# Layer 0 experts: the next expert's gathered rows are transposed and split in steps, one behind each column block of the first product

## The chip, the core and the metric

The kernel runs on one NeuronCore of a Trainium2 chip. The metric is device time in microseconds (us) for one launch; a lower time is better. The engines are PE (matmul), ACT (ScalarE), DVE (VectorE), POOL (GpSimd, here the issuer of gathers and scatters) and SP (SyncE, here the issuer of plain loads). Each runs its own list of instructions in order and waits on the others by semaphores.

## What is computed

The program is a two-layer backbone: per layer a mixer (attention and a second branch) and then an expert-choice feed-forward. Layer 0 serves a latent stream of 1024 tokens and a context stream of 256; layer 1 serves the latent stream alone. The change lies in the experts of layer 0:

```python
def expert_choice_ffn(h, w_router, w1, w3, w2):
    n_tok, d = h.shape[1], h.shape[2]
    cap = EC_FACTOR * n_tok // N_EXPERTS
    aff = jax.nn.softmax(jnp.einsum('bnd,de->bne', h, w_router).astype(jnp.float32), axis=-1)
    gate, idx = lax.top_k(jnp.swapaxes(aff, 1, 2), cap)
    xs = jax.vmap(lambda hb, ib: hb[ib])(h, idx)
    a = jnp.einsum('becd,edf->becf', xs, w1)
    b = jnp.einsum('becd,edf->becf', xs, w3)
    y = jnp.einsum('becf,efd->becd', jax.nn.silu(a) * b, w2) * gate[..., None].astype(h.dtype)
```

There are 16 experts. Each takes the 128 latent tokens (and, in layer 0, 32 context tokens) that score highest for it; the model and the hidden width are 1024. The results are added back to the rows they came from.

## The kernel before

Every fp32 operand is held as two fp16 halves, high and low, and each product is three matmuls (`mm3`, L146 to L148). A weight piece of 128 x 2048 is loaded as fp32 (`raw`, 1 MB, issued by SP in `slab`, L442) and split: ACT writes the high half (L102), DVE the low half (L103), into `spl`. An expert has twelve such pieces, here numbered 0 to 11 in the order of their splits: 0 to 3 and 4 to 7 are w1 and w3 for the first and second half of the hidden columns, 8 to 11 are w2. In layer 0 `raw` has four buffers, used in turn, so the load of piece n can start only when DVE has split piece n - 4. `spl` has ten, so the split of piece n waits until PE is done with piece n - 10. The splits therefore run some six pieces ahead of PE.

`experts` (L458) loops over the experts. For one expert of layer 0 the work on PE is

- the first product in four column blocks, called block 1 to 4 here: per block 48 matmuls into `pa` (w1) and 48 into `pb` (w3), each with 160 columns (128 latent and 32 context tokens). Behind a block ACT and DVE form silu(a) times b (`sa`, L547 and L548) and split it into `gh` (ACT, L114) and `gl` (DVE, L116);
- the second product, 48 matmuls of 512 columns into `y` for the latent tokens (eight hidden blocks k, two halves, three passes), and 48 of four concurrent column groups into `yc` for the context tokens (L590). What follows a matmul with `gl` of block 4 needs that block's split;
- the scaling of `y` into `ysb` (DVE, L572) and the scatters (POOL, L579 and L596).

While one expert runs, `fetch` prepares the next one's input: POOL gathers 128 rows into `xs` (L474, two buffers) and 32 rows into `xc` (L479, one buffer). PE transposes `xs` in two groups of four (`tr`, L160), and `xc` in one group of eight (`trc`, L489). ACT applies the norm's gain and shift to each group while it reads it from PSUM into `xv` (`affine`, L509), and `split_a` makes `xsh` (ACT, L114) and `xsl` (DVE, L116) of it. All three groups go through one PSUM buffer (tag `tr`, one buffer in layer 0) and one buffer `xv`, so a group's transposes cannot start before ACT has read the group ahead.

`fetch` is called once for each expert, in the second half of the hidden columns, ahead of block 3:

```python
                w1, w3 = ws[:2], ws[2:]
                if fh and e + 1 < NE:
                    nxt = fetch(e + 1)
```

The order of the instructions on each engine is not that of the program text: a scheduler with a timeline model of its own places them, with the text's order as priority. So a change of the text at one place can change the order anywhere behind it.

Of the kernel before, what the change touches and what calls it, by code (L numbers as in the profile page):

```python
# [26 lines left out]
NE = 16  # L27
# [28 lines left out]
def weave(*streams):  # L56
    """streams: (generator, expected sum of its yields, start); advances the one that is least far, start and length 1 being
    where and how fast it runs against the others; a stream that yields a function waits until it is true"""
    live = [[st[0], 0.0, float(st[1]), st[2] if len(st) > 2 else 0.0, None] for st in streams]
    while live:  # L60
        s = min((v for v in live if v[4] is None or v[4]()), key=lambda v: v[3] + v[1] / v[2])
        try:
            r = next(s[0])
            s[4] = r if callable(r) else None
            s[1] += 0.0 if callable(r) else r
        except StopIteration:
            live.remove(s)


class Tag:  # L70
    """one tag of a pool with a fixed number of buffers"""
# [8 lines left out]
class Net:  # L80
# [10 lines left out]
    def first(self, g, n):  # L91
        """the generator's instructions before the n traced ahead of them that are ready too"""
        while True:
            with self.tc.high_priority(n):
                r = next(g, None)
            if r is None:
                return
            yield r

# [5 lines left out]
    def load_split(self, src, n, sp, raws, step=1024):  # L105
        """src [128, n] in DRAM -> sp [128, 2, n]"""
# [32 lines left out]
    def stats(self, x, n, junk, tag):  # L139
        """1 / rms of the rows; tag: buffers of its own for each caller that runs beside others"""  # L140
        ss = self.small.tile([P, 1], F32, name="ss" + tag, bufs=2)
        self.S.activation(junk, x, AF.Square, accum_out=ss)
        return self.rstd_of(ss, n, tag)
# [6 lines left out]
    def turn(self, dst, src):  # L150
        """dst [128, n, 128] <- the n blocks of src [128, n * 128] transposed, 2-byte elements"""
        return self.Y.dma_start(dst, src, transpose=True)

    def trans(self, src, n, psum, w=P):
        """src [128, n*w] fp32 -> psum tiles [w, 4, 128]"""
# [34 lines left out]
    def behind(self, ins):  # L190
        """what is traced inside is issued after ins, on its engine"""
        return contextlib.nullcontext() if ins is None else self.tc.issue_after(ins)

    def mod_bank(self, l, i, psum, raws, last=None, n=1024):
        """rows 32g + stream of the bank: columns 512(4i + g) of the modulation of layer l; n: columns of a load"""
# [24 lines left out]
    def mod_cols(self, l, i, g0, psum):  # L220
        """chunks g0, g0 + 1 of a bank with the model's dimension on partitions: psum [128, 4, 128], columns 32(g0 + g) + stream"""
        return self.trans(self.modsb[l, i], 4, psum)[0]

    def mod_AB(self, l, which, psum):
        """per-partition gain and shift [128, 8] of the norm before the mixer (1) or before the experts (2)"""
# [19 lines left out]
    def router(self, l, j, A, B, psum):  # L245
        """router weights with the norm's gain in them, and the row that its shift gives"""
# [12 lines left out]
    def mod_bc(self, l, m, j, dst, psum):  # L259
        """row m of the modulation for stream j on all partitions, over WS"""  # L260
# [7 lines left out]
    def norm_T(self, src, l, j, hi, lo, xs, psum):  # L268
        """hi, lo: [128, 8, 128] views"""
# [18 lines left out]
    def tail(self, l, j, t, src, catT, wout, m2, xd, h2d, aff, psum, c4, t2, cn=None, xin=None, ptr=None):  # L288
        """catT: k -> (hi, lo) [128, 128 tokens]; wout: (k, half) -> (hi, lo); yields its tensor-engine time"""
# [55 lines left out]
    def topk(self, src, n, cap, tag, off=0, alt=None, bufs=0):  # L345
        """largest cap of src [16, n] in falling order and their columns plus off; src is used up; alt: a second buffer, which
        lets the search for columns run beside the next round"""
# [20 lines left out]
    def merge(self, r, l):  # L368
        """largest 128 of two falling lists of 128; on equal values the first list wins"""
# [10 lines left out]
    def slots(self, vals, idf, cap, psum, halves):  # L380
        """per slot: row index and gate [slots, 16]; halves: also the index of half rows, for both halves"""
# [25 lines left out]
    def ring(self, raws, spls, first=()):  # L407
        """buffers for the experts' weights as loaded and split, (pool, tag) of each, no pool: self.ep; first: those for the first loads"""
# [13 lines left out]
    def first_slabs(self, l, a, b):  # L422
        """loads of the weights a .. b before the tokens are chosen"""
# [7 lines left out]
    def split_first(self, a, b, last=None):  # L431
        """their split, beside VectorE, which the choice holds; not before the instruction last"""
# [9 lines left out]
    def slab(self, src, a):  # L442
        """128 x 2048 weights, split: two views [128, a, 2048 / a]"""
# [14 lines left out]
    def experts(self, l, xd, h2d, lat, ctx, hook=None, keep=None, out=None):  # L458
        """lat = (idx, gate, _); ctx = (xdc, h2dc, (idx, gate, idx2)) or None"""
# [7 lines left out]
        def halves(name, i, e):  # L467
            """[128, 8, N] for expert e, in self.ep or in a buffer of the pool keep"""
# [3 lines left out]
        def fetch(e):  # L472
# [3 lines left out]
            xc = None  # L476
            if ctx:
                xc = ep.tile([P, D], F32, name="xc", bufs=1)
                G.indirect_dma_start(out=xc[:CCAP], out_offset=None, in_=ctx[1], in_offset=IOA(ap=ctx[2][0][:CCAP, e:e + 1], axis=0))  # L479
            for h in range(2):  # L480
# [4 lines left out]
                self.split_a(v, hi[:, sl, :CAP], lo[:, sl, :CAP])  # L485
            if ctx:
# [6 lines left out]
            return hi, lo  # L493
# [17 lines left out]
        def rows(fh, w1, w3, xh, xl, gh, gl):  # L511
            """512 of the hidden columns with the tokens on partitions, then transposed and split"""
# [12 lines left out]
        nxt = fetch(0)  # L525
        for e in range(NE):
            xh, xl = nxt
            gh, gl = halves("gh", 2, e), halves("gl", 3, e)
            for fh in range(2):
                ws = [slab(I[n][l, e, fh, kh], 4) for n in ("w1", "w3") for kh in range(2)]  # L530
                w1, w3 = ws[:2], ws[2:]
                if fh and e + 1 < NE:
                    nxt = fetch(e + 1)
                if ctx is None:
                    rows(fh, w1, w3, xh, xl, gh, gl)
                    continue
                for fp in range(2):
# [12 lines left out]
                    self.split_a(sa, gh[:, fsl], gl[:, fsl])  # L550
            if hook and e == NE - 3:
# [48 lines left out]
    def norm_out(self, xs, fg, tag):  # L600
        """the rows of the tiles over their rms, times the gain, in place"""
# [16 lines left out]
    def even(self, xd, xdc, h2d, h2dc, then):  # L618
        nc, tc, V, S, T, G, Y, I = self.nc, self.tc, self.V, self.S, self.T, self.G, self.Y, self.I
        with self.pool("m0") as pm, self.pool("m0p", PSUM) as pp:  # L620
# [56 lines left out]
            def ropes(ps, H, t):  # L677
                """rotated [128, H, 64] fp32, scale undone by the table"""
# [75 lines left out]
            def score(keep, u):  # L754
                """scores of the unit's heads, a bank for each run of blocks, and the transposed probabilities"""
# [38 lines left out]
            def values():  # L794
                """the oldest unit's probabilities times values; after a tile's last ones its heads' outputs"""
# [108 lines left out]
            def att_all():  # L904
                """the scores run two units ahead of the values"""
# [69 lines left out]
    def odd(self, ms, mw, xs, xsc, xd, h2d, W, then):  # L975
# [9 lines left out]
        if True:  # L985
# [4 lines left out]
            def ropes(z, H, t, b):  # L990
                """z [128, H, 32] view, rotated in place"""
# [14 lines left out]
            if True:  # L1006
                with self.pool("m1c") as pc, self.pool("m1cp", PSUM) as pp:
# [20 lines left out]
                    def lowrank(hh, hl, i, t, lat):  # L1028
# [13 lines left out]
                        def low(parts, r, g, n, tag, dst):  # L1042
                            """n columns normalized, split and transposed into dst"""
# [59 lines left out]
            with self.pool("m1zp", PSUM) as pz:  # L1103
# [3 lines left out]
                def conv_all():  # L1107
                    """gated short convolution, channels on partitions; then the output weights"""
# [52 lines left out]
                if True:  # L1161
# [24 lines left out]
                    def score(t, h, i):  # L1186
                        """scores of a head against one block of keys; after the last one the probabilities"""
# [41 lines left out]
                    def values():  # L1229
                        """the oldest block of probabilities times values; after a tile's last one its heads' outputs"""  # L1230
# [20 lines left out]
                    def att_all():  # L1251
                        """the scores run LA heads ahead of the values"""
# [32 lines left out]
                    def tails():  # L1285
                        """output products and what follows, each tile's buffer for its rows in one of two tags"""
# [128 lines left out]
def pack(x, c, ctx, c_ctx, mod_w, mod_b, norm1_g, norm2_g, ev_w_in, ev_sink, ev_sgu_norm_g, ev_sgu_w, ev_sgu_b, ev_w_out, od_w_in,  # L1415
# [5 lines left out]
    def kpack(w, kt):  # L1421
        """[kt*128, n] -> [128, kt*n]"""
# [54 lines left out]
```

## Time and profile before

| | us |
|---|---|
| median of 3 runs | 2750.52 |
| lowest and highest run | 2747.89, 2755.91 |
| span of the profiled execution, first to last instruction | 2750.4 |
| PE busy | 2361.6 (86%) |
| DVE busy | 2036.0 (74%) |
| ACT busy | 1678.1 (61%) |
| POOL busy | 337.3 (12%) |

No other time is given for the profiled execution than its span; it lies 0.1 us under the median. The program falls into stages: modulation and the layer 0 mixer up to about 700 us, the experts of layer 0 from there to 1428 us, the mixer of layer 1 to about 2165 us, and the experts of layer 1 to the end. A share of busy time over the whole span mixes these.

### The profile page before, as it was taken

What the parts mean: (1) busy time and instruction counts of PE and PEld (TensorE: products, weight loads), DVE (VectorE), ACT (ScalarE), POOL (GpSimd) and SP (SyncE); (2) the same over time, 40 slices, a digit from 0 to 9 for tenths busy, and PEclk for the clock granted to TensorE, in tenths of its full rate; (3) what the DMA queues carried; (4) which work ended last, traced back from release to release, by engine and by line L of the source; (5) the groups of instructions that cost most, each with busy time, mean ns of one, the idle gap of its engine ahead of it and who ended that gap; (6) DMA issues with size and microseconds to landing.
All of it is one profiled execution on the core that took longest, in us unless ns stands there. A gap on an engine that the chain in (4) does not pass through costs nothing. (4 is left out here: it accounts for less than half of the span.)

```text
span 2750.4 us, 48542 instructions
## 1 busy us (share of the span) xinstructions
PE 2361.6 (86%) x19075; PEld 1436.0 (52%) x19075; DVE 2036.0 (74%) x3886; ACT 1678.1 (61%) x2750; POOL 337.3 (12%) x198
## 2 busy tenths in 40 slices
PE   5889888864899999999989989988884699999995
PEld 1345555432677777776855645544553244444442
DVE  5466666676677777767857768778778789888887
ACT  4355556514666676767745456656554588777774
POOL 1000000003111111111120000000015111112211
PEclk8999999886899999999999999999986799999998
DMA  8775555473788888887967657878876499999997
GB/s 309 218 171 118 123 106 117 93 260 112 267 307 285 323 286 322 289 319 272 352 204 225 147 124 142 152 137 186 162 187 244 181 371 401 361 366 360 373 370 273
DMA packets 461995, 661.32 MB, mean 240 GB/s; under 512 B 371115, under 2 KB 371419, under 8 KB 411077
## 3 DMA queue, kind: packets, MB, share of 16 engines
q1 hardware_dynamic: 439894, 582.81, 66.8%
q0 software_dynamic: 21872, 75.41, 9.4%
q8 instruction: 149, 2.44, 0.4%
q14 instruction: 80, 0.66, 0.1%
HBM read 526.86 MB, written 41.94 MB: 207 GB/s over the span
## 5 line engine op out<-in xcount | busy, mean ns | idle before, releaser
L103 DVE SCALAR_TENSOR_TENSOR spl<-raw,spl 128x2048 f16<-128x2048 f32 x369 | 831.7, 2285 | 149.4 <-ACT spl L102 148.8
L102 ACT ACTIVATE spl<-raw 128x2048 f16<-128x2048 f32 x369 | 690.5, 1910 | 191.7 <-DMA raw<-in_w 73.0
L146 PE MATMUL pb<-xsh,spl 128*128 128x160 f16 x1024 | 222.6, 239 | 0.0
L148 PE MATMUL pb<-xsh,spl 128*128 128x160 f16 x1024 | 222.2, 239 | 0.0
L147 PE MATMUL pb<-xsl,spl 128*128 128x160 f16 x1024 | 222.1, 239 | 0.0
L146 PE MATMUL pa<-xsh,spl 128*128 128x160 f16 x1024 | 215.9, 234 | 0.0
L147 PE MATMUL pa<-xsl,spl 128*128 128x160 f16 x1024 | 215.7, 234 | 0.0
L148 PE MATMUL pa<-xsh,spl 128*128 128x160 f16 x1024 | 215.6, 234 | 0.0
L146 PEld LDWEIGHTS <-spl 128*128 128x128 f16 x2048 | 204.0, 100 | 7.2 <-PE yc L590 5.1
L148 PEld LDWEIGHTS <-spl 128*128 128x128 f16 x2048 | 204.2, 100 | 0.2
L147 PEld LDWEIGHTS <-spl 128*128 128x128 f16 x2048 | 204.0, 100 | 0.2
L146 PE MATMUL y<-spl,gh 128*128 128x512 f16 x512 | 195.2, 383 | 10.2 <-ACT gh L114 10.2
L147 PE MATMUL y<-spl,gh 128*128 128x512 f16 x512 | 195.1, 382 | 0.0
L148 PE MATMUL y<-spl,gl 128*128 128x512 f16 x512 | 189.3, 385 | 4.9 <-DVE gl L116 4.9
L579 POOL DMA_INDIRECT xd<-ysb,idxl x31 | 125.4, 4044 | 529.2 <-DVE ysb L572 503.6
L1212 ACT ACTIVATE pr<-sps,nm 128x512 f32<-128x512 f32 (+1 forms) x192 | 116.7, 611 | 104.2 <-DVE nm L1203 79.5
L146 PE MATMUL po<-vS,pT 128*128 128x64 f16 x976 | 121.9, 198 | 56.7 <-DMA pT<-ps 34.6
L1195 PE MATMUL sps<-kT,qT 128*128 128x512 f16 (+1 forms) x576 | 133.7, 352 | 11.6 <-ACT pr L1212 11.2
L146 PEld LDWEIGHTS <-pT 128*128 128x128 f16 x976 | 92.1, 101 | 89.9 <-DMA pT<-ps 48.6
L1196 DVE TENSOR_REDUCE mx<-sps 128x1 f32<-128x512 f32 (+1 forms) x192 | 112.6, 596 | 33.9 <-PE sps L1195 30.9
L116 DVE TENSOR_TENSOR ps<-pr,ps 128x512 f16<-128x512 f32 (+1 forms) x192 | 111.8, 595 | 34.6 <-ACT ps L114 34.4
L213 PE MATMUL modps<-mslab,cs 128*2 128x512 f32 x384 | 89.4, 681 | 53.1 <-DMA mslab<-in_mod_w 48.6
(439 smaller groups left out, 5957.1 us busy)
## 6 DMA issues: line engine op xcount, KB each, us to landing
raw<-in_w SPq DMA_DIRECT2D x384, 1024.0 KB, 7.6
mslab<-in_mod_w SPq DMA_DIRECT2D x80, 512.0 KB, 5.8
mslab<-in_mod_w SPq DMA_DIRECT2D x8, 1024.0 KB, 9.5
raw<-in_wz SPq DMA_DIRECT2D x12, 512.0 KB, 6.7
raw<-in_wconv SPq DMA_DIRECT2D x24, 256.0 KB, 3.6
xin<-in_x POOLq DMA_DIRECT2D x8, 512.0 KB, 6.1
raw<-in_ev_wo SPq DMA_DIRECT2D x8, 512.0 KB, 3.9
xres<-in_x POOLq DMA_DIRECT2D x8, 512.0 KB, 5.3
```

The source lines that it names most:

```text
L102: self.S.activation(hi, raw, AF.Copy, scale=scale)
L103: self.V.scalar_tensor_tensor(lo, raw, scale, hi, op0=OP.mult, op1=OP.subtract)
L116: self.V.tensor_tensor(lo, src, hi, OP.subtract)
L146: self.T.matmul(ps, lh, rh, start=first, stop=False)
L147: self.T.matmul(ps, lh, rl, start=False, stop=False)
L148: return self.T.matmul(ps, ll, rh, start=False, stop=last).ins
L213: T.matmul(ps[c0:c0 + 2], lhs, slab[:rows, g * 512:(g + 1) * 512], start=False, stop=(k == 8), tile_position=(0, c0))
L579: G.indirect_dma_start(out=xd, out_offset=IOA(ap=lat[0][:, e:e + 1], axis=0), in_=ysb, in_offset=None, compute_op=OP.add)
L1195: T.matmul(ps[:, :w], qT[:, 4 * j + h % 4], kT[:, k, c0:c0 + w], start=j == 0, stop=j == 2)
L1196: V.tensor_reduce(mx[:, i:i + 1], ps[:, :w], axis=AX.X, op=OP.max)
L1212: S.activation(pr[:, :w], sp[i][:, :w], AF.Exp, bias=nm, scale=SC1, accum_out=dn[:, i:i + 1])
```

## The change

`fetch` becomes a generator with four steps: the two gathers, the first group of `xs`, the second group of `xs`, the group of `xc`. The loop makes it when an expert starts and takes one step behind each of the four column blocks. In layer 1 (`ctx is None`) it is still drained in one go at the old place. The change also drops docstrings and comments, so the line numbers of the two versions differ by up to seven (L509 becomes L511, L489 L492, L548 L554, L572 L579).

```diff
-        def fetch(e):
+        def fetch(e, got):
+
             xs = ep.tile([P, D], F32, name="xs", bufs=2)
             G.indirect_dma_start(out=xs, out_offset=None, in_=h2d, in_offset=IOA(ap=lat[0][:, e:e + 1], axis=0))
             hi, lo = halves("xsh", 0, e), halves("xsl", 1, e)
-            xc = None
+            got.append((hi, lo))
             if ctx:
                 xc = ep.tile([P, D], F32, name="xc", bufs=1)
                 G.indirect_dma_start(out=xc[:CCAP], out_offset=None, in_=ctx[1], in_offset=IOA(ap=ctx[2][0][:CCAP, e:e + 1], axis=0))
+            yield
             for h in range(2):
                 ps, = self.trans(xs[:, h * 512:(h + 1) * 512], 4, ztr)
                 v = ep.tile([P, 4, P], F32, name="xv", bufs=1)
                 affine(ps, v, 0, 4 * h, 4, CAP)
                 sl = slice(4 * h, 4 * h + 4)
                 self.split_a(v, hi[:, sl, :CAP], lo[:, sl, :CAP])
+                yield
             if ctx:
                 ps = ztr([P, 8, CCAP], "trc")
...
                 self.split_a(v, hi[:, :, CAP:], lo[:, :, CAP:])
-            return hi, lo
...
-        nxt = fetch(0)
+        got = []
+        for _ in fetch(0, got):
+            pass
         for e in range(NE):
-            xh, xl = nxt
+            xh, xl = got.pop(0)
             gh, gl = halves("gh", 2, e), halves("gl", 3, e)
+            nxt = fetch(e + 1, got) if e + 1 < NE else iter(())
             for fh in range(2):
                 ws = [slab(I[n][l, e, fh, kh], 4) for n in ("w1", "w3") for kh in range(2)]
                 w1, w3 = ws[:2], ws[2:]
-                if fh and e + 1 < NE:
-                    nxt = fetch(e + 1)
                 if ctx is None:
+                    if fh:
+                        for _ in nxt:
+                            pass
                     rows(fh, w1, w3, xh, xl, gh, gl)
                     continue
                 for fp in range(2):
...
                     self.split_a(sa, gh[:, fsl], gl[:, fsl])
+                    next(nxt, None)
```

What it does to the order, for one expert in the steady run of the stage. The first place is PE in the first product: the second group `tr` and the group `trc`. Before, and now:

```order
L147 LDWEIGHTS spl
L147 MATMUL pb<-xsl,spl 128x160
L160 MATMUL tr<-c_ident,xs 128x128 x4
L148 LDWEIGHTS spl
L148 MATMUL pb<-xsh,spl 128x160
...
L148 MATMUL pb<-xsh,spl 128x160
L489 MATMUL trc<-c_ident,xc 128x32 x8
L146 LDWEIGHTS spl
L146 MATMUL pb<-xsh,spl 128x160
```

```order
L148 LDWEIGHTS spl
L148 MATMUL pb<-xsh,spl 128x160
L160 MATMUL tr<-c_ident,xs 128x128 x4
L146 LDWEIGHTS spl
L146 MATMUL pa<-xsh,spl 128x160
...
L148 LDWEIGHTS spl
L148 MATMUL pb<-xsh,spl 128x160
L492 MATMUL trc<-c_ident,xc 128x32 x8
L146 LDWEIGHTS gh
L146 MATMUL y_10042<-spl,gh 128x512
```

The first group stands behind block 2 in both. The second stood 65 matmuls later, inside `pb` of block 3, and now stands 96 matmuls later, behind block 3. `trc` stood 12 matmuls into `pb` of block 4 and now stands behind block 4, ahead of `y`.

The second place is ACT over the same stretch, from the splits of piece 11 and of the next expert's piece 0 on. Before, and now:

```order
L102 ACTIVATE spl<-raw 128x2048 x2
L509 ACTIVATE xv<-tr,B_911,A_912 128x128 x4
L102 ACTIVATE spl<-raw 128x2048
L114 ACTIVATE gh<-sa 128x320
L114 ACTIVATE xsh<-xv 128x4x128
L547 ACTIVATE sa<-pa 128x320
L509 ACTIVATE xv<-tr,B_911,A_912 128x128 x4
L114 ACTIVATE gh<-sa 128x320
L102 ACTIVATE spl<-raw 128x2048
```

```order
L102 ACTIVATE spl<-raw 128x2048 x2
L511 ACTIVATE xv<-tr,B_911,A_912 128x128 x4
L114 ACTIVATE gh<-sa 128x320
L102 ACTIVATE spl<-raw 128x2048
L553 ACTIVATE sa<-pa 128x320
L114 ACTIVATE xsh<-xv 128x4x128
L114 ACTIVATE gh<-sa 128x320
L511 ACTIVATE xv<-tr,B_911,A_912 128x128 x4
L102 ACTIVATE spl<-raw 128x2048
```

The two splits still stand ahead of the first `xv`. Block 2's `gh` moves ahead of the next split, and block 3's `gh` ahead of the second `xv`.

The third place is DVE, from the same splits to `gl` of block 4. Before, and now:

```order
L103 SCALAR_TENSOR_TENSOR spl<-raw,spl 128x2048 x3
L116 TENSOR_TENSOR gl<-sa,gh 128x320
L116 TENSOR_TENSOR xsl<-xv,xsh 128x4x128
L548 SCALAR_TENSOR_TENSOR sa<-pb,sa 128x320
L116 TENSOR_TENSOR gl<-sa,gh 128x320
L103 SCALAR_TENSOR_TENSOR spl<-raw,spl 128x2048
L116 TENSOR_TENSOR xsl<-xv,xsh 128x4x128
L548 SCALAR_TENSOR_TENSOR sa<-pb,sa 128x320
L103 SCALAR_TENSOR_TENSOR spl<-raw,spl 128x2048 x3
L116 TENSOR_TENSOR gl<-sa,gh 128x320
```

```order
L103 SCALAR_TENSOR_TENSOR spl<-raw,spl 128x2048 x2
L116 TENSOR_TENSOR gl<-sa,gh 128x320
L103 SCALAR_TENSOR_TENSOR spl<-raw,spl 128x2048
L554 SCALAR_TENSOR_TENSOR sa<-pb,sa 128x320
L116 TENSOR_TENSOR xsl<-xv,xsh 128x4x128
L116 TENSOR_TENSOR gl<-sa,gh 128x320
L103 SCALAR_TENSOR_TENSOR spl<-raw,spl 128x2048
L554 SCALAR_TENSOR_TENSOR sa<-pb,sa 128x320
L103 SCALAR_TENSOR_TENSOR spl<-raw,spl 128x2048
L116 TENSOR_TENSOR xsl<-xv,xsh 128x4x128
L103 SCALAR_TENSOR_TENSOR spl<-raw,spl 128x2048 x2
L116 TENSOR_TENSOR gl<-sa,gh 128x320
```

The same 14 instructions stand there in another order: seven splits, three `gl`, two `xsl`, two `sa`. POOL's order does not change, and SP's loads of the expert weights do not either. In the mixer of layer 1 the scheduler also gives another order: PE, ACT, DVE and SP interleave the scores, the values, the queries and the convolution otherwise from the attention on, with the same instructions. In the last experts of layer 1 a few transposes stand some matmuls earlier or later.

## Rows read from the trace of the kernel before

**Rows 1.** The page: span, busy times, and granted clock in 40 slices.
```profile
span 2750.4 us, 48542 instructions
PE 2361.6 (86%) x19075; PEld 1436.0 (52%) x19075; DVE 2036.0 (74%) x3886; ACT 1678.1 (61%) x2750; POOL 337.3 (12%) x198
PEclk8999999886899999999999999999986799999998
```
**Rows 2.** Busy time by window: experts 0, attention of layer 1, experts 1.
```profile
core 0: us, PE busy (x) PEld busy (x) DVE busy (x) ACT busy (x) POOL busy (x), PEclk, DMA share, GB/s
720.00:1380.00 660.00, 622.99 (x7134) 497.07 (x7133) 497.70 (x395) 464.20 (x590) 108.31 (x55) 0.98 0.85 306
1590.00:2045.00 455.00, 407.05 (x3613) 230.86 (x3612) 346.20 (x907) 287.13 (x712) 5.33 (x10) 0.95 0.77 152
2165.00:2705.00 540.00, 517.73 (x2463) 245.73 (x2462) 466.37 (x298) 416.65 (x394) 96.35 (x28) 0.98 0.97 364
```
**Rows 3.** Waits from 720 to 1380 us: total, times, longest.
```profile
ACT spl L102 <- DMA raw<-in_w: 59.9, 22, 4.9
...
PE tr L160 <- ACT xv L509: 37.0, 13, 3.6
```
**Rows 4.** Timeline of PE: the first group of transposes, experts 1 and 14.
```profile
758.84 0.49 PE L160 MATMUL tr<-c_ident,xs 128*128 128x128 f32 x3
...
1360.18 0.60 PE L160 MATMUL tr<-c_ident,xs 128*128 128x128 f32 x4
```
**Rows 5.** Timeline of PE through one expert (start, length, what, [idle before]).
```profile
886.58 0.24 PE L146 MATMUL pa<-xsh,spl 128*128 128x160 f16 x1
...
899.87 0.60 PE L160 MATMUL tr<-c_ident,xs 128*128 128x128 f32 x4
...
903.63 0.23 PE L146 MATMUL pb<-xsh,spl 128*128 128x160 f16 x1
...
907.73 0.66 PE L160 MATMUL tr<-c_ident,xs 128*128 128x128 f32 x4 [2.76 <-ACT xv L509]
908.22 0.23 PE L148 MATMUL pb<-xsh,spl 128*128 128x160 f16 x1
...
914.61 0.68 PE L489 MATMUL trc<-c_ident,xc 32*128 32x32 f32 x8
...
917.72 0.38 PE L146 MATMUL y<-spl,gh 128*128 128x512 f16 x1
...
928.28 0.39 PE L148 MATMUL y<-spl,gl 128*128 128x512 f16 x1
...
930.11 0.39 PE L590 MATMUL yc<-spl,gl 128*32 128x512 f16 x1
...
931.73 0.24 PE L146 MATMUL pa<-xsh,spl 128*128 128x160 f16 x1
```
**Rows 6.** Timeline of ACT in the same expert.
```profile
902.58 3.71 ACT L102 ACTIVATE spl<-raw 128x2048 f16<-128x2048 f32 x2 [4.06 <-DMA raw<-in_w]
906.19 1.49 ACT L509 ACTIVATE xv<-tr,B,A 128x128 f32<-128x128 f32 x4
907.56 1.92 ACT L102 ACTIVATE spl<-raw 128x2048 f16<-128x2048 f32 x1
909.36 0.47 ACT L114 ACTIVATE gh<-sa 128x320 f16<-128x320 f32 x1
```
**Rows 7.** Timeline of DVE in the same expert.
```profile
919.81 6.68 DVE L103 SCALAR_TENSOR_TENSOR spl<-raw,spl 128x2048 f16<-128x2048 f32 x3
926.41 0.48 DVE L116 TENSOR_TENSOR gl<-sa,gh 128x320 f16<-128x320 f32 x1
```
**Rows 8.** Windows as in rows 2: behind two waits of PE, and this expert.
```profile
862.20:865.60 3.40, 3.40 (x29) 3.40 (x27) 2.90 (x4) 1.69 (x4) 0.89 (x1) 0.50 1.00 414
907.80:911.20 3.40, 3.40 (x48) 3.39 (x49) 2.90 (x2) 2.88 (x4) 1.21 (x1) 1.00 0.95 345
886.58:931.73 45.15, 42.39 (x498) 33.61 (x497) 34.29 (x28) 31.87 (x41) 6.95 (x5) 1.00 0.85 306
```

## The prediction

> **What bounds the kernel now.** I read the page first: PE is busy 86% of a span of 2750.4 us and DVE 74% [rows 1]. That is a mean over stages with different limits, so I took windows next. In the stage that the change touches, the experts of layer 0, PE is busy 623.0 of 660 us, DVE 497.7, ACT 464.2, and the DMA engines 0.85 of the time at 306 GB/s; in the experts of layer 1 the same engines move 364 GB/s at 0.97 [rows 2]. So in layer 0 PE is nearest to its limit, and the loads have room. The view of waits then says what PE waits for there: 13 waits for ACT's `xv`, 37.0 us in all and 3.6 at most, and no other wait of PE of that size [rows 3].
>
> The timelines of one expert show how that wait comes about. Call the start of block 1 time 0 (886.58). PE issues the first group of transposes at 13.29 and would reach the second after a few matmuls more, but stands still for 2.76 us until 907.73, 21.15 on that clock [rows 5]. The second group needs the only PSUM buffer, which ACT empties into `xv`. ACT was late: it waited 4.06 us for a load (piece 11), began that split at 902.58 (16.00), did two splits, and only then `xv`, which ends at 907.68 (906.19 + 1.49) [rows 6]. So PE's wait ends 5.1 us behind the landing of piece 11, whatever PE does in between. That load starts when DVE has split piece 7, early in the same expert.
>
> The waits have a second price. Behind one of them the granted clock is 0.50, that is 1.2 GHz in place of 2.4, and PE is busy all through; behind another, of 2.76 us, it is 1.00 [rows 8]. A stretch of 3.40 us at 0.50 loses 1.7 us of work. From the first group of expert 1 (758.84) to that of expert 14 (1360.18) there are 13 experts in 601.34 us, 46.26 each [rows 4]. PE's own work is 42.39 us in an expert without a fall of the clock [rows 8]. 13 x 42.39 = 551.1, and the 13 waits are 37.0; the 13.3 that remain I put down to the clock.
>
> **The change, part by part.** *Instructions.* None is added or removed on any engine; DMAs are the same, POOL's order too. Only places change, and the order says how.
>
> *First group of transposes:* behind block 2, as before. 0 us.
>
> *Second group.* It now stands behind all of block 3. A `pa` or `pb` takes 3.32 us (from `pb` at 903.63 back to the end of the transposes at 900.31, which start at 899.87 and take 0.44 of issue) [rows 5]. So PE reaches it at 13.29 + 0.44 + 6.64 = 20.37. `xv` is over at 21.10 if ACT's list ahead of it is unchanged, which the order says: the same two splits stand there. The wait is then 21.15 - 20.37 = 0.78 us and not 2.76. Its bounds are 0 (the load comes 0.8 us sooner) and 2.76 (it comes 2.0 later). I take 0.78, as nothing ahead of that load moves by more than a `ysb`.
>
> *The group of `xc`.* It waits for the second `xv`. ACT now has block 3's `gh` ahead of that, which waits for DVE's `sa`, and DVE has the split of the next expert's piece 1 ahead of that `sa`. From ACT's and DVE's rows: `gh` of block 2 takes 0.36 of ACT, the split ends 1.92 later [rows 6], DVE's split 2.2 more (a third of 6.68) [rows 7], `sa`, `xsl` and `xv` some 2.5: the second `xv` ends at about 28.1. PE is done with block 4 at 21.15 + 0.49 + 6.64 = 28.28. No wait, but with 0.2 us to spare; bounds 0 and 1.
>
> *The second product.* This is where the next wait appears. PE needs 0.61 for `trc` and reaches `y` at 28.9, 2.2 us sooner than before (31.14, 917.72) [rows 5]. The last eight matmuls of `y` need `gl` of block 4, which DVE finishes at 926.41 + 0.48 = 926.89, time 40.31, the last of a list that began with the split of piece 11 and holds seven splits [rows 7]. Before, PE came there at 928.28 (41.70), 1.4 us after it [rows 5]. DVE's list from piece 11 to this `gl` holds the same 14 instructions, so I leave its end at 40.31 and allow 0.5 either way for its order. PE now comes at 28.9 plus what lay between `y` and the last eight before (928.28 - 917.72 = 10.56) plus 0.1 for two more `yc` ahead of them: 39.56. New wait: 40.37 - 39.56 = 0.81 us, bounds 0 and 1.5. The cover is thus gone: from here an expert is bound by load, ACT and DVE, not by PE.
>
> *The end of the expert.* Eight `y` take 930.11 - 928.28 = 1.83 and the remaining 23 `yc` about 1.5 (25 took 1.62) [rows 5]: 40.37 + 1.83 + 1.5 = 43.70, against 45.15 before. The mean wait of the 13 is 37.0 / 13 = 2.85 [rows 3], 0.09 more than here, so piece 11 lands that much later on the mean: 43.8.
>
> *The clock.* Before, waits of up to 3.6 us [rows 3] let it fall in some experts. I take it that two waits of 0.8 us, some 19 us apart, leave it at 2.4 GHz: the wait of 2.76 at 907.73 did so already [rows 8]. The other bound is a fall in every expert. It costs 1.7, of which 0.81 goes into the wait for `gl` that follows, so 0.89 x 13 = 11.6 us.
> The Trainium skill's page "TensorE: Matmul & The Clock Gate", section "A second HAM failure mode: psum-queue depth-cycling", tells of a kernel that went through PSUM buffers with small pauses between groups of matmuls, often enough that the clock swung between its levels. That speaks against this change, which puts two small pauses where one long one was; by that rule the sum would end 11.6 us higher. No row read here shows what the clock does behind a wait under 1 us.
>
> *POOL and the scatters.* The gather of `xc` waits for `trc`, now some 0.9 us later in an expert's time, and the scatter of `ysb` is queued behind it. That scatter needs the last `y` anyway, 13 us later. 0 us.
>
> *First and last experts.* Expert 14 had no such wait and expert 15 fetches nothing; expert 0 fetches early in both orders. 0, within 1 us.
>
> *The mixer of layer 1.* Its order changes though its text does not. PE idles 455.0 - 407.05 = 48 us in the attention [rows 2]. Work and dependencies are the same, so the bounds are what the idle time allows: 48 gained, and as much lost if it doubled. I take 0, with 8 us (a sixth of that idle time) either way, as the late parts stand at the same places among the scores in both orders. The experts of layer 1 run at 0.97 of the DMA engines [rows 2], and a few transposes moved by some matmuls do not change their loads: 0.
>
> **Sum.** 13 x (46.26 - 43.8) = 32.0 us, 13.3 of it clock and the rest waits. 2750.4 - 32.0 = 2718.4, and as the median lies 0.1 above the profiled span, **2718.5 us**.
>
> **The rivals.** *PE alone is the limit* (12%): piece 11 lands sooner or DVE's new order ends sooner, and neither wait is left. Then 13 x (46.26 - 42.39) = 50.3 us go: 2700.1. For it: the loads have room [rows 2]. Against: ACT still waits 59.9 us for loads in this stretch [rows 3], and nothing in the change makes them start earlier.
>
> *The clock still falls* (15%): 2718.5 + 11.6 = 2730.1, as worked out above.
>
> *The loads close up* (14%): the new order puts a split between the two halves of `ysb`, so the scatter starts about 2.2 us later and meets the loads of pieces 10 and 11, and an expert's loads have 2.4 us less time. Each us that piece 11 lands later costs an expert 1 us. At 1.5 us later, 2718.5 + 13 x 1.5 = 2738.0; at 2.46 later nothing is gained at all. Against: 0.85 of the DMA engines' time over 45.15 us [rows 8] is 38.4 us, which still goes into 43.8.
>
> *Slower: the attention of layer 1* (6%). Its PE idle time of 48 us nearly doubles under the new interleaving, by 45: 2718.5 + 45 = 2763.5. It decides from 40.3 us of loss on (the 32.0 and 8.3 more). For it: nobody chose that order. Against: the same instructions and the same places for the late work.
>
> That the change does not do what it says is out: the order shows each group behind its block.
>
> **How the numbers follow.** My own case has 47%, and its range, with 8 us for layer 1 and the half us of DVE's order, is 2710 to 2727; 6% is left for mixtures that I did not work out. About 0.3% (8.3 us) is what a measurement of this kernel can tell from no change, so "faster" is below 2742.3 and "slower" above 2758.8. Faster: 46 of my own case, 12, 14 of the clock's 15, 8 of the loads' 14, 3 of the rest: 83%. Same: 10% (5 of the loads, 3 of the rest, 2 of others). Slower: 7% (6 of the attention, 1 of the loads). The range of 2698 to 2741 reaches from just under the case of PE alone to the loads at 1.7 us later.
>
> **What would show it.** Right: the waits of the second group for `xv` fall to about 0.8 us each (some 10 us in all); a wait of PE in `y` for `gl` of about 0.8 appears; 43.8 us from one first group to the next; the split of piece 11 still begins at 16 us; the granted clock in this stage at 0.99 or more; and 1590 to 2045 shifted by 32 us and as long as before. Wrong: second-group waits still above 2 us, piece 11 landing at 17.5 or later, a clock of 0.97 or less, or an attention stage longer by more than 10 us.

## The result, and the profile after

The changed kernel takes 2714.11 us (median of 4 runs, 2708.74 to 2715.35), the kernel before 2752.49 in the same set. The ratio is 0.9843, with a 95% interval of 0.9823 to 0.9862: 38.4 us faster, 4.4 us below the forecast of 2718.5 and inside the range. The profiled execution has a span of 2713.5 us.

The page of the changed kernel, to set against [rows 1]:

```profile
span 2713.5 us, 48543 instructions
PE 2346.0 (86%) x19075; PEld 1421.8 (52%) x19075; DVE 2033.3 (75%) x3886; ACT 1680.0 (62%) x2750; POOL 323.8 (12%) x198
PEclk7999999886899999999989999998985799999998
```

Busy time by window in the changed kernel, as [rows 2]: the experts of layer 0, the attention of layer 1 and the experts of layer 1 (both shifted by about 35 us), and last one single expert.

```profile
core 0: us, PE busy (x) PEld busy (x) DVE busy (x) ACT busy (x) POOL busy (x), PEclk, DMA share, GB/s
720.00:1350.00 630.00, 611.65 (x7187) 486.91 (x7185) 500.43 (x397) 469.88 (x590) 97.07 (x55) 1.00 0.89 322
1555.00:2010.00 455.00, 405.62 (x3611) 228.96 (x3612) 351.81 (x916) 286.91 (x713) 5.33 (x10) 0.95 0.77 152
2131.00:2671.00 540.00, 520.15 (x2482) 246.95 (x2481) 468.05 (x299) 416.35 (x396) 93.96 (x29) 0.99 0.97 364
790.78:834.00 43.22, 42.24 (x497) 33.52 (x497) 34.21 (x28) 32.19 (x41) 6.95 (x4) 1.00 0.89 321
```

The two stages of layer 1 are what they were. In layer 0 the granted clock is now 1.00, and PE idles 18.4 us in 630 where it idled 37.0 in 660. The view of waits from 720 to 1350 us says which waits went and which came:

```profile
ACT spl L102 <- DMA raw<-in_w: 65.5, 30, 4.6
...
PE y L148 <- DVE gl L116: 7.2, 11, 0.7
...
PE tr L160 <- ACT xv L511: 5.3, 7, 1.4
...
PE pb L148 <- DVE spl L103: 2.8, 2, 1.9
...
PE trc L492 <- ACT xv L511: 1.2, 1, 1.2
```

The 37.0 us for `xv` [rows 3] are 5.3; 7.2 us for `gl`, 11 waits of at most 0.7, are new; the some 6 that remain of the 18.4 lie in experts 13 and 14. ACT's own waits for loads did not shrink (59.9 before, 65.5 now): they are as long, but much less of PE's time hangs on them.

From the first group of expert 1 to that of expert 14, as [rows 4], there are now 565.08 us, 43.47 per expert where there were 46.26:

```profile
762.10 0.49 PE L160 MATMUL tr<-c_ident,xs 128*128 128x128 f32 x3
...
1327.18 0.38 PE L160 MATMUL tr<-c_ident,xs 128*128 128x128 f32 x2
```

The timeline of PE through one expert, as [rows 5], with the start of block 1 at 790.78:

```profile
790.78 0.24 PE L146 MATMUL pa<-xsh,spl 128*128 128x160 f16 x1
...
804.07 0.60 PE L160 MATMUL tr<-c_ident,xs 128*128 128x128 f32 x4
...
811.55 0.66 PE L160 MATMUL tr<-c_ident,xs 128*128 128x128 f32 x4 [0.25 <-ACT xv L511]
...
818.78 0.68 PE L492 MATMUL trc<-c_ident,xc 32*128 32x32 f32 x8
...
830.76 0.61 PE L148 MATMUL y<-spl,gl 128*128 128x512 f16 x2 [0.73 <-DVE gl L116]
...
834.00 0.24 PE L146 MATMUL pa<-xsh,spl 128*128 128x160 f16 x1
```

The timelines of ACT and of DVE in the same expert, as [rows 6, 7]:

```profile
806.40 3.71 ACT L102 ACTIVATE spl<-raw 128x2048 f16<-128x2048 f32 x2 [3.69 <-DMA raw<-in_w]
810.01 1.49 ACT L511 ACTIVATE xv<-tr,B,A 128x128 f32<-128x128 f32 x4
...
825.82 4.49 DVE L103 SCALAR_TENSOR_TENSOR spl<-raw,spl 128x2048 f16<-128x2048 f32 x2
830.23 0.48 DVE L116 TENSOR_TENSOR gl<-sa,gh 128x320 f16<-128x320 f32 x1
```

ACT still waits for piece 11 (3.69 us) and splits it from 15.62 on, still does two splits ahead of `xv`, and `xv` still ends 5.1 us behind the landing of piece 11 (810.01 + 1.49 - 806.40). PE now comes there at 20.4 and waits 0.25, not 2.76. The last `gl` ends at 830.71, 24.31 us behind the start of piece 11's split, and PE waits 0.73 for it.

### The profile page after: what moved, and what is told of

Read it like the earlier page. It is cut to its first block, busy times and chain, and to the rows that moved or that the text cites. A ratio compares the mean times of both kernels' runs of the same rounds, so it can differ in the third digit from the quotient of the medians.

```text
span 2713.5 us, 48543 instructions
## 1 busy us (share of the span) xinstructions
PE 2346.0 (86%) x19075; PEld 1421.8 (52%) x19075; DVE 2033.3 (75%) x3886; ACT 1680.0 (62%) x2750; POOL 323.8 (12%) x198
## 5 line engine op out<-in xcount | busy, mean ns | idle before, releaser
L148 PE MATMUL pb<-xsh,spl 128*128 128x160 f16 x1024 | 214.2, 233 | 2.8 <-DVE spl L103 2.8
L146 PE MATMUL pb<-xsh,spl 128*128 128x160 f16 x1024 | 214.4, 233 | 0.0
L147 PE MATMUL pb<-xsl,spl 128*128 128x160 f16 x1024 | 214.2, 233 | 0.0
L146 PEld LDWEIGHTS <-spl 128*128 128x128 f16 x2048 | 200.5, 98 | 6.5 <-issue 5.9
L148 PEld LDWEIGHTS <-spl 128*128 128x128 f16 x2048 | 200.3, 98 | 3.2 <-DVE spl L103 3.2
L147 PEld LDWEIGHTS <-spl 128*128 128x128 f16 x2048 | 200.4, 98 | 0.3
L586 POOL DMA_INDIRECT xd<-ysb,idxl x31 | 115.4, 3723 | 533.4 <-DVE ysb L579 508.9
L1202 PE MATMUL sps<-kT,qT 128*128 128x512 f16 (+1 forms) x576 | 133.0, 354 | 13.3 <-ACT pr L1219 10.8
L146 PEld LDWEIGHTS <-pT 128*128 128x128 f16 x976 | 92.2, 101 | 91.1 <-DMA pT<-ps 48.2
```

What stands on the lines that cost most here:

```text
L146: self.T.matmul(ps, lh, rh, start=first, stop=False)
L147: self.T.matmul(ps, lh, rl, start=False, stop=False)
L148: return self.T.matmul(ps, ll, rh, start=False, stop=last).ins
L586: G.indirect_dma_start(out=xd, out_offset=IOA(ap=lat[0][:, e:e + 1], axis=0), in_=ysb, in_offset=None, compute_op=OP.add)
L1202: T.matmul(ps[:, :w], qT[:, 4 * j + h % 4], kT[:, k, c0:c0 + w], start=j == 0, stop=j == 2)
```

## Where the 38 us came from

Busy time by window over the twelve steady experts, 1 to 12, from the start of a block 1 to the start of another: first in the kernel before (all twelve, then one in which the clock fell), then in the changed kernel.

```profile
745.55:1300.28 554.73, 520.08 (x5954) 414.73 (x5953) 413.22 (x326) 383.45 (x483) 94.17 (x49) 0.98 0.83 301
745.55:792.29 46.74, 43.98 (x497) 35.15 (x496) 34.36 (x28) 31.86 (x41) 8.33 (x5) 0.96 0.82 299
```

```profile
748.81:1266.14 517.33, 506.06 (x5956) 402.22 (x5953) 410.52 (x323) 386.11 (x482) 80.51 (x48) 1.00 0.89 322
```

By the medians the kernel gained 38.4 us; the two profiled executions, on which this part rests, lie 36.9 apart. The twelve take 37.4 us less (46.23 each before, 43.11 now). PE's idle time went from 554.73 - 520.08 = 34.65 to 11.27, which is 23.4 of it; PE's busy time fell by 14.0. Most of the 14.0 is the clock: the expert at 745.55 has the same wait of 2.76 as the one of [rows 5], but the clock falls in it (0.96), and PE is busy 43.98 and not 42.39 [rows 8], so a fall costs 1.59. Seven of the twelve took 46.7 us or more, the other five 45.4 or less: 7 x 1.59 = 11.1. The 2.9 that remain, 0.24 per expert, go with the order of PE's list: in the first run below, where that list is the old one again, PE is busy 42.38 us in an expert with the clock at 1.00 (842.92 to 888.04), as before. Which place in the order it is stays open.

The stage as a whole, from its first `pa` to its last `yc`, is 33.9 us shorter (725.48 to 691.56), because expert 13 took 46.7 as before and expert 14 lost 3.6 us. The two in the kernel before, to set against those of the changed kernel (shown with the run on the weights of layer 1):

```profile
1300.28:1346.89 46.61, 44.24 (x497) 35.12 (x496) 37.65 (x33) 35.58 (x45) 6.17 (x4) 0.96 0.90 325
1346.89:1388.64 41.75, 41.75 (x500) 33.69 (x497) 36.86 (x29) 33.18 (x42) 5.51 (x2) 1.00 0.96 349
```

The rest of the difference lies outside the stage: it began 3.4 us later, and what follows it was 6.4 us shorter. The same changed kernel in a second profiled execution began the stage 4.1 us sooner (701.87 for 706.01), so parts of this size are what two executions differ by.

## The experiments

Theory A: PE's old wait came from the order on ACT. `xv`, which frees the one PSUM buffer, stood behind two splits that a load held up, and PE came for the buffer too early. After the change PE comes later, and what is left is set by the list of ACT and DVE from piece 11 to the last `gl`. Rivals: C, the gain is from the earlier gathers or the new order elsewhere; D and G, PE alone or the loads' own pace sets the expert. Each ratio is to runs of the kernel before in the same set. That kernel's median was between 2750 and 2760 us in the sets, so times of different sets compare by their ratios.

**The steps put together again.**

```diff
             for h in range(2):
                 ps, = self.trans(xs[:, h * 512:(h + 1) * 512], 4, ztr)
...
-                yield
+            yield
```

> The changed kernel with both groups of xs in one step behind block 2 again; the gathers (behind block 1) and the group of xc (a step of its own, here behind block 3) stay as changed. Theory A (the old wait came from PE reaching the second group of transposes before ACT, held by the load of piece 11, had emptied the one PSUM buffer): PE stands 2.5 to 3 us at the second group of each expert again, the clock falls behind some of these waits, an expert takes 46 us again, 2740 to 2755 us in all. Rival C (the gain comes from the earlier gather, or from the new order of ACT, DVE or of layer 1): an expert stays at 43 us and the time at 2714, within 6.

Measured: 2754.26 us, ratio 1.0013 [0.9994, 1.0031]. Waits from 720 to 1380 us, and the window of the same twelve experts:

```profile
PE tr L160 <- ACT xv L511: 34.3, 13, 3.6
```

```profile
749.10:1300.40 551.30, 518.48 (x5953) 413.30 (x5953) 413.17 (x326) 383.67 (x483) 92.98 (x49) 0.98 0.84 303
```

All of the gain is gone: 45.9 us per expert, 13 waits at the second group, the clock at 0.98. PE's list in an expert is the old one again: the second group 65 matmuls behind the first, and `trc` 12 into `pb` of block 4, though it is still a step of its own. So the effect lies in this order; both groups went back, and the waits, 13 at the second group, say which of them it is. The earlier place of the gathers in the text is not it: the gather of `xs` waits for `tr` in all three kernels, and starts 22.08 us into the expert before, 21.71 in the changed kernel and 22.06 here.

**The old wait removed on ACT's side, in the kernel before.** ACT's splits of piece 11 and of the next piece 0 get an ordering edge to the `xv` of the first group (`behind` issues what is traced inside it after a given instruction of its engine). `fetch` stays in one go.

```diff
-            self.split_w(raw, sp[:, 0], sp[:, 1])
+            with self.behind(last): self.split_w(raw, sp[:, 0], sp[:, 1])
...
-            w2 = [slab(I["w2"][l, e, q], 2) for q in range(4)]
+            w2 = [slab(I["w2"][l, e, q], 2, self.xv1 if ctx and q == 3 and e + 1 < NE else None) for q in range(4)]
```

(`self.xv1` is the last instruction of that `xv`; the slab of the next expert's first piece gets the same edge.)

> The kernel before, fetch in one go as it was; only ACT's splits of piece 11 and of the next expert's piece 0 are made to stand behind the xv of the first group. Theory A: ACT empties the buffer before it waits for the load, the 37 us of waits at the second group go without any step being moved behind a block, and what is left is set by the landing of piece 11: 43 to 44 us per expert, 2710 to 2725 us. Rival C (the steps between the blocks, or the earlier gather, are what gains): 46 us per expert, 2750 us, within 6.

Measured: 2709.86 us, ratio 0.9857 [0.9834, 0.9881]. The window of twelve experts, and ACT and DVE in one of them (block 1 starts at 961.87):

```profile
750.47:1257.83 507.36, 507.36 (x5953) 402.43 (x5953) 412.16 (x325) 387.35 (x482) 98.34 (x48) 1.00 0.91 328
```

```profile
975.86 1.50 ACT L509 ACTIVATE xv<-tr,B,A 128x128 f32<-128x128 f32 x4 [2.05 <-PE tr L160]
977.25 3.72 ACT L102 ACTIVATE spl<-raw 128x2048 f16<-128x2048 f32 x2
...
998.61 0.48 DVE L116 TENSOR_TENSOR gl<-sa,gh 128x320 f16<-128x320 f32 x1
```

PE is busy 507.36 of 507.36 us: 42.28 per expert and no wait at all, though no step was moved behind a block. The scheduler changed PE's list too, but so that PE comes to the second group sooner and not later: it now stands 43 matmuls behind the first, not 65 (`trc` moved into `y`). PE still waits for nothing there, as `xv` is over at 15.49 and not at 21. That settles the cause of the old wait. The expectation of 43 to 44 us was too high: I had taken the landing of piece 11 for the next limit. It starts its split at about the same time here (15.4), but the list from there to the last `gl` takes 21.84 us (999.09 - 977.25) and not 24.31, as `xv` (1.5 us) no longer stands in it. So `gl` is over at 37.22, ahead of PE, which comes to the last eight matmuls of `y` at 39.04:

```profile
1000.91 0.39 PE L148 MATMUL y<-spl,gl 128*128 128x512 f16 x1
```

This kernel's expert 13 took 48.2 us, with one wait of 3.1 for `xv`.

**Half of piece 11 loaded.**

```diff
-            self.Y.dma_start(raw, src)
...
+            if half:
+                self.Y.dma_start(raw[:, :1024], src[:, :1024])
+                r2 = raw[:, :1024].unsqueeze(1).broadcast_to([P, 2, 1024])
...
```

> The changed kernel with only half of piece 11 (the last w2 piece of an expert of layer 0) loaded; both halves of its split are made of that half, so ACT, DVE and PE do the same work. It leaves out half of the last two hidden blocks' w2 weights. Theory A (now the landing of piece 11 sets the expert, over ACT's and DVE's lists to the last gl): the landing comes 1 us or more sooner, the new waits for gl go, an expert falls from 43.1 to 42.1 to 42.5, PE's own work: 2700 to 2708 us. Rival D (PE's work alone sets the expert already): 2714, within 4.

Measured: 2721.36 us, ratio 0.9897 [0.9869, 0.9926], slower than the changed kernel, which neither theory expected. ACT and PE in one expert (block 1 starts at 789.07):

```profile
803.97 5.51 ACT L102 ACTIVATE spl<-raw 128x2048 f16<-128x2048 f32 x3 [2.96 <-DMA raw<-in_w]
809.39 1.48 ACT L516 ACTIVATE xv<-tr,B,A 128x128 f32<-128x128 f32 x4
...
810.93 0.66 PE L160 MATMUL tr<-c_ident,xs 128*128 128x128 f32 x4 [1.32 <-ACT xv L516]
```

Piece 11 did come sooner (its split starts at 14.90, not 15.62), and no wait for the last `gl` is left. But the scheduler now put three splits ahead of `xv`, not two, so `xv` ended at 21.80 and the wait at the second group was back at 1.32 us, 13.1 in 12 waits from 745 to 1340 us. I had changed two things with one edit, and the run says nothing on the landing. It agrees with the run before in that PE's wait grows with the splits ahead of `xv`.

**The weights of layer 1.** At expert 13 a hook sends eight loads for the mixer of layer 1 through the same `raw` buffers.

```diff
-            if hook and e == NE - 3:
-                hook(self.raw)
             w2 = [slab(I["w2"][l, e, q], 2) for q in range(4)]
+            if hook and e == NE - 1:
+                hook(self.raw)
```

> The changed kernel with the eight loads and splits of layer 1's first weights (3.8 MB) issued behind the weights of expert 15, not ahead of the last four pieces of expert 13. Theory A (an expert is as long as its loads make it, so these 3.8 MB are why experts 13 and 14 took 46.7 and 45.3 us): both fall to 43.1, and the loads lie in the stretch in which expert 15 has nothing more to load: 2706 to 2710 us. Rival F: the mixer of layer 1 waits for these weights, up to the 12 us that 3.8 MB take at 306 GB/s: 2714 to 2722 us.

Measured: 2704.78 us, ratio 0.9833 [0.9811, 0.9854]. The windows of experts 13 and 14 in the changed kernel, and then in this one:

```profile
1266.14:1312.83 46.69, 42.36 (x500) 33.68 (x497) 36.87 (x33) 35.33 (x46) 5.94 (x3) 1.00 0.88 302
1312.83:1358.15 45.32, 42.56 (x499) 33.52 (x497) 38.95 (x30) 35.20 (x43) 6.42 (x2) 1.00 0.97 346
```

```profile
1264.89:1307.81 42.92, 42.20 (x500) 33.55 (x497) 34.21 (x28) 32.27 (x41) 5.74 (x3) 1.00 0.87 314
1307.81:1350.41 42.60, 42.04 (x500) 33.49 (x497) 34.22 (x28) 31.98 (x41) 4.79 (x2) 1.00 0.87 312
```

92.0 us became 85.5: the 3.8 MB are why these two experts were longer. The whole time says less: the ratios, 0.9843 and 0.9833, differ by some 3 us and their intervals overlap. The mixer is not held up: from the last `yc` of layer 0 to the first scores of layer 1 it took 170.9 us, 172.7 before the move. F falls, and the time is a little under the range of A.

**Three combinations.** The first two join edits shown above. ACT's order in the kernel before, with the hook last:

> The kernel before (fetch in one go) with the two ACT splits behind the first xv, as in the run that did only this, and with layer 1's first weights issued behind the weights of expert 15. Theory A: 42.28 us per expert throughout, PE's own time, and experts 13 and 14 take 42 each and no longer 48.2 and 39.8; 2700 to 2706 us. Rival F (those 3.8 MB then hold up the mixer of layer 1): 2710 to 2720 us.

Measured: 2696.13 us, ratio 0.9783 [0.9745, 0.9821], 4 us under the range expected. Then the same two edits on the changed kernel:

> The changed kernel with layer 1's first weights behind those of expert 15 (2704.8 us alone) and also with ACT's splits of piece 11 and of the next piece 0 behind the first xv. Theory A, sharpened (what holds an expert at 43.1 us is ACT's and DVE's list from the split of piece 11 to the last gl, 24.3 us, in which xv costs 1.5): the list gets shorter by 1.5 to 2.5 us, the last gl comes before PE needs it, 42.0 to 42.4 us per expert, 2690 to 2697 us. Rival G (the loads' own pace holds the expert at 43.1): 2705, within 4.

Measured: 2704.64 us (2698.32 to 2717.58), ratio 0.9825 [0.9777, 0.9873]: this median lies where G had it and not in the range of A, but the runs scatter too much for it to decide. The profiles, of 2693.6 and 2697.5 us, are clear. Fourteen experts in the first kernel, and then in the second, with ACT and DVE in one expert (block 1 starts at 1003.28):

```profile
745.16:1337.08 591.92, 591.92 (x6946) 469.49 (x6945) 480.24 (x378) 450.12 (x561) 109.76 (x53) 1.00 0.91 328
```

```profile
748.95:1342.38 593.43, 593.43 (x6948) 469.20 (x6945) 479.38 (x378) 449.02 (x561) 103.03 (x54) 1.00 0.92 327
...
1017.27 1.51 ACT L511 ACTIVATE xv<-tr,B,A 128x128 f32<-128x128 f32 x4 [2.05 <-PE tr L160]
1018.78 3.71 ACT L102 ACTIVATE spl<-raw 128x2048 f16<-128x2048 f32 x2
...
1037.67 0.49 DVE L116 TENSOR_TENSOR gl<-sa,gh 128x320 f16<-128x320 f32 x1
```

PE never waits in either, 42.28 and 42.39 us per expert. The list from piece 11 to the last `gl` takes 19.4 us in the second, 4.9 less than in the changed kernel. So that list, and not the pace of the loads, held the changed kernel at 43.1: G falls, as 12 MB an expert arrive in 42.4 us too. With ACT's order put right, the steps between the blocks gain nothing more in these profiles.

Third, a fifth `raw` buffer in the changed kernel, with the hook last:

```diff
-                self.ring(own[1:4] + [(None, "raw")], ...
+                self.ring(own[2:4] + [(None, "raw"), (None, "raw4")] + own[1:2], ...
...
-            xs = ep.tile([P, D], F32, name="xs", bufs=2)
+            xs = ep.tile([P, D], F32, name="xs", bufs=1 if ctx else 2)
...
-            if ctx:
-                xc = ep.tile([P, D], F32, name="xc", bufs=1)
...
+                if h and ctx:
+                    xc = ep.tile([P, D], F32, name="xc", tag="xs", bufs=1)
```

> The changed kernel with layer 1's first weights behind those of expert 15 (2704.8 us alone) and a fifth raw buffer; the room for it comes from gathering xc into the one buffer of xs behind block 3. ACT still does two splits ahead of the first xv. Theory A (load n waits for split n - 4, so the landing of piece 11 is set by a buffer that comes free late): with split n - 5 in its place the load starts 2.2 to 2.8 us sooner, ACT does not wait at piece 11, no wait at the second group or for the last gl is left, 42.0 to 42.4 us per expert, 2690 to 2697 us. Rival G (the loads' own pace holds the expert at 43.1): 2705, within 4. Rival H (the gather of xc, now behind the second group, comes late for its transposes): PE waits at trc, 2705 or more.

Measured: 2694.46 us (2687.69 to 2709.34), ratio 0.9779 [0.9727, 0.9831]. Fourteen experts, and PE's waits in them:

```profile
751.27:1338.67 587.40, 585.55 (x6945) 470.79 (x6944) 479.60 (x378) 447.42 (x561) 103.56 (x56) 1.00 0.94 332
```

```profile
PE tr L160 <- ACT xv L511: 1.8, 4, 0.7
```

41.96 us per expert. ACT still waits 0.7 to 2.3 us for piece 11, not zero as expected, but that is short enough. H falls here: `trc` stands 22 matmuls into `y`, and the gather is in time. The least that PE's work takes depends on where the pieces are interleaved: 41.7 here in an expert without a wait, 42.3 and 42.4 above.

**All three edits** in one kernel, with no new line, and beside it the changed kernel as it is:

> The changed kernel with all three edits: five raw buffers, ACT's splits of piece 11 and of the next piece 0 behind the first xv, and layer 1's first weights behind those of expert 15. Theory A: no wait for ACT, DVE or a load is left in an expert, and PE's own work is all that remains, 41.7 to 42.4 us by the two runs that had these edits one at a time; the stage is 20 us shorter than in the changed kernel (15 experts, 1.3 us each), ratio to the kernel before 0.975 to 0.980. Rival G (with all buffers and orders right, the loads of 12 MB an expert or contention of ACT and DVE come forward as the next limit): 43 us an expert, ratio 0.982 or more.

> The changed kernel as it is, beside the next run on the same chip, so that the two can be compared: ratio to the kernel before 0.9843 as in the first measurement, within 0.002.

Measured: 2714.10 us, ratio 0.9836 [0.9812, 0.9860], and 2714.37 us, ratio 0.9838 [0.9815, 0.9861], for the changed kernel, which repeats its first measurement. A miss for A. The ratio is one that G gave, but no wait of PE for a weight load, ACT or DVE is left, so G is not the reason. PE's waits in fourteen experts, and one of them on PE:

```profile
PE trc L492 <- DMA xc<-hc,idxc: 7.3, 10, 2.2
```

```profile
1201.65 0.53 PE L492 MATMUL trc<-c_ident,xc 32*128 32x32 f32 x6 [2.19 <-DMA xc<-hc,idxc]
```

It is rival H, which I had dropped after the run before: the scheduler placed `trc` 9 matmuls into `y` and not 22, and the late gather of `xc` now came too late in most experts. The fourteen experts take 597.3 us (744.84 to 1342.14) where the kernel with five buffers and the hook last took 587.4: more idle time makes 5.7 of the 9.9 us, and PE is busy 4.2 longer, part of it one fall of the clock. By the ratios (0.9836 against 0.9779) this kernel is some 16 us behind, but those intervals overlap. The profiled execution took 2702.12 us, 12 less than this kernel's median, and where its other runs lost that is open.

**The first of the combinations again**, unaltered. It and the one with five buffers are the fastest here, 0.9783 and 0.9779, and the runs do not tell them apart:

> Again the kernel before with ACT's two splits behind the first xv and layer 1's first weights behind those of expert 15, to compare it with the changed kernel in more runs. Theory A: ratio to the kernel before 0.977 to 0.981, against 0.984 of the changed kernel, the difference being 0.8 us in each of 12 experts and 7 us in experts 13 and 14. Against it: 0.982 or more, no better than the changed kernel.

Measured: 2703.45 us, ratio 0.9800 [0.9776, 0.9825]. With 0.9783 before, it takes some 2% less than the kernel before and is ahead of the changed kernel (0.9843, 0.9838) in both measurements, by some 0.4% to 0.6%; the intervals overlap at their ends, but for one pair. The stage is steadier than the total: from its first `pa` to its last `yc` it took 675.1 and 675.2 us in the two profiled executions, whose spans differ by 9.7, and 691.6 and 690.3 in those of the changed kernel. `fetch` stays in one go in it.

## Why the prediction was right, and where it was off

- *The cause of the wait.* Right, and shown from both sides: the wait returns when the second group returns to its place, and it goes when ACT is made to empty the buffer first.
- *Second group.* Forecast 0.78 us each, some 10 in all; measured 5.3 in 7 waits. Piece 11's split starts at 15.6 us on the mean (the eleven experts in which PE waited for `gl`) and not at 16.1. Why is argued and not shown: in DVE's new order a split stands ahead of the second `ysb` half, so the load of piece 10 starts at 1.03 and not 1.48, but that of piece 11 itself starts at 3.90 and not 3.68. With the scatter later, the loads moved 2.41 MB in the first 9 us of the expert shown and POOL's transfers 0.07, where it was 1.37 and 0.42 in the expert of [rows 5]. The rival by which the later scatter delays these loads came out the other way round.
- *The group of `xc`.* Forecast no wait, with 0.2 us to spare: right, but for one wait of 1.2 in expert 13.
- *The new wait for `gl`.* Forecast 0.81 us; measured 0.65 on the mean, 11 times. That an expert is then bound by ACT's and DVE's list and not by PE was right for the changed kernel, and the runs with the list shortened show it.
- *The expert.* Forecast 43.8 us; measured 43.11 over the twelve steady ones, so the twelve gained 37.4 and not 12 x 2.46 = 29.5. Of the 0.69 us per expert 0.5 is the earlier piece 11 and 0.1 is expert 1, which took 41.97 without a wait; the 24.3 us from there to the last `gl` stood as forecast (16.00 to 40.31).
- *The clock.* Forecast 13.3 us back. The price of a fall was 1.59 (taken as 1.7), and there were eight falls in the stage, 12.7 us. The granted clock is 1.00 in 720 to 1350 us: two waits of up to 1.1 us in an expert, time after time, did not make it fall, and the rival of 11.6 us did not come. The Trainium skill ("TensorE: Matmul & The Clock Gate", section "A second HAM failure mode: psum-queue depth-cycling") tells of small repeated pauses that let the clock swing; these did not.
- *Experts 13 and 14.* This step failed. Expert 13 was counted among those that gain, 2.46 us, and gained nothing; "0, within 1 us" for expert 14 was a loss of 3.6. I had looked at their waits in the trace of before and not at what else their loads carry: the 3.8 MB for layer 1 go through the same buffers there, and with the experts shorter there is less time to hide them. Moving them shows it. Together with the better steady experts this leaves the stage at -33.9 for a forecast of -32.0: the gain was forecast 7.9 us too small for the twelve and 6.1 too large for these two, and the two misses all but cancel. That the sum came so close is in part luck.
- *Layer 1.* Forecast 0, within 8: measured 6.4 us shorter from the last `yc` on in one pair of executions, 4.5 of it ahead of the first scores. Two executions of one kernel (the first of the combinations) differ there by 2.8 us in all, and by 6.7 in the attention alone; whether the new order has a part in it, no run tells.

## What to carry to other kernels

When PE waits for a buffer that another engine has to empty, look at what stands ahead of the emptying instruction in that engine's list: if it is work held by a load, an ordering edge that puts it behind may do what moving PE's work does, and more. Before a gain per iteration is multiplied, read each iteration's own length and look for the ones that carry extra transfers. And when a scheduler orders the instructions, read its new order before an experiment is believed: an edit meant only to shorten a load moved a third split ahead of `xv`, and one that joined three gains brought a wait back.

## What the runs showed of the hardware that was not expected

The granted clock did not follow the length of the wait alone. In the kernel before it fell behind one wait of 2.76 us and not behind another of 2.76; it fell in expert 13 with a wait of 2.37 (0.96 in its window, shown above) and stayed in expert 6 with one of 3.02:

```profile
978.62:1024.02 45.40, 42.38 (x497) 33.59 (x497) 34.28 (x28) 31.86 (x41) 6.96 (x5) 1.00 0.85 306
```

In the second execution of the changed kernel it fell in expert 13 behind a wait of 2.06 us (0.96 from 1260.14 to 1308.44). In the run with half of piece 11 waits of up to 2.0 us left it at 1.00 over the twelve experts. In the run with all three edits the expert with the 2.19 us wait for `xc` had it at 0.96, by this window from the start of its block 1 to the next:

```profile
1169.91:1215.80 45.89, 43.70 (x500) 33.85 (x497) 34.51 (x27) 31.97 (x41) 9.62 (x5) 0.96 0.88 306
```
